# Hybrid attention and retention block: transposes on another engine, background work on another timetable, four multiplies on another engine

## The chip, the cores and the metric

The kernel runs on one core of one Trainium2 chip. The core has five engines that each work through their own queue in order and meet only at semaphores: TensorE (PE, with its weight loads shown as PEld), VectorE (DVE), ScalarE (ACT), GpSimd (POOL) and SyncE (SP, which here only issues DMAs). The metric is the device time of one execution in microseconds. Before the change the median of three runs was 1860.13 us (1857.83 to 1861.78).

## The reference, cut to what matters

One layer over 512 tokens of width 2048, float32. All mixing is causal by chunks of 64 tokens.

```python
h = rmsnorm(x, norm_gain)
proj = h @ w_in
(aq, ak, av, az, iq, ik, iw, rq, rk, rv, rz, ga, gb) = jnp.split(proj, SPLIT_POINTS, axis=-1)
...
# mixer A: an indexer scores all keys, 128 of them are kept for each query
index = jnp.einsum('bqsh,bqh->bqs', jax.nn.relu(score), w_c)
_, sel = lax.top_k(index, topk)
bias = rel_table[t5_bucket(pos_sel - pos_c[:, :, None])]
logits = jnp.einsum('bqhd,bqkhd->bqkh', q_c, k_sel) * scale + bias
...
# mixer B: retention, 8 heads of 128, chunkwise recurrent
kv = jnp.einsum('bnkhd,bnkhe->nbhde', kc * to_end[:, :, None], vc)
y = ((y - mu) * lax.rsqrt(var + EPS)).reshape(B, L, R_WIDTH) * gn_gain
...
a_out = dsa_mixer(...) * jax.nn.silu(az)
b_out = retention_mixer(rq, rk, rv, ret_gn_gain) * jax.nn.silu(rz)
merged = jax.nn.sigmoid(ga) * (a_out @ w_a_out) + jax.nn.sigmoid(gb) * (b_out @ w_b_out)
r = x + merged @ w_o
return r + (p_i @ w_ple) * jax.nn.sigmoid(r @ w_ple_gate)
```

The top-k is computed without indices: sixteen rounds, each of which finds the eight largest scores of a row and overwrites them; what was overwritten is kept, and the rest gets a large negative number in `mneg`. The position bias is computed from 32 masks per query group (position difference against a threshold) that are multiplied by a small table on PE.

## The kernel before

**Numbers.** Every float32 product is made of three products of a rounded high part and a remainder: `wh` and `wl` for weights (ACT rounds at L134, DVE or POOL subtracts at L140), `hh` and `hl` for activations. POOL subtracts for the weights of retention and of attention (`pool_units`), DVE for all others. So each 1024 columns of weights cost one ACT pass and one pass of DVE or POOL ahead of PE.

**Order.** The program order of every engine is written out by hand. PE's matmuls set the pace: after each group of three (or two) matmuls the code calls `step()`, one *tick*, which may issue other work at that point of the program. Three lists feed it: `soon` holds work due a given number of ticks later (`later(n, f)`), `todo` is a list of slots, one taken per tick, where `None` is an empty slot, and `bg` is background work. A background piece is issued in a tick when `todo` has run empty and the tick's number is a multiple of `state["rate"]`.

**Background pieces, 256 in this order.** 48 that load `x` again, normalize it (`xn`) and write the 56 sums and parts of it that the paired products use to `hd` in DRAM (`h_step`, L264 to L277); 48 top-k pieces, sixteen rounds over three query tiles of 256, 384 and 512 keys (`topk_round`, L601 and L602 on DVE, with `mneg` at the end); 160 for the bias: 128 `bias_mask` (L616, DVE) and 32 `bias_mm` (twelve matmuls, L624, an ACT copy, and a store to `scr` that ACT issues).

**Stages, in order.** The indexer's projections. Then `values` for four retention heads (64 ticks) and four heads; again `values` and four heads. A head has two projections, `ps_rq` and `ps_rk`, of 16 ticks each. `rotate` (L714 to L717, four DVE operations) follows each, and the head's remaining work goes onto `todo` only behind the second one, so that it is issued beside the next head's projections: `scores` (L747, PE; then `at`, L749, DVE), `keys` (16 stream transposes on DVE in four slots, then an ACT copy with a scale, L759), `states` (L764, PE), four `values_out` (L778 and L780, PE), `norm` (L785 to L790, DVE, and a power on POOL), `scale` (`yn`, L797, DVE), `back` (16 stream transposes, then an ACT copy with the gain, L807, and a store by SP to `yd`). Only the last head has both projections in one loop, which also reads the parts in `hd` back (`x_load`). Behind it stands gate pair 0.

22 gate pairs follow (`gemm_pair`: `rz`, `gb`, `ga` and half of `az`). A pair computes two output blocks of 128 columns with seven products of eight ticks (56 ticks) into four PSUM tiles p, v, q and r; p, v and r are used twice, so that the sixth and seventh product wait until DVE and ACT have read them (`e_d`, L229, reads r ahead of the seventh). The weights of a pair are four loads by SP and three additions by DMA that POOL issues into the loaded tile. Then branch B's projection with `w_b` (16 blocks of 8 ticks, L895), where `x` is split again on the way (`x_again`, with three empty slots behind each). Then `av` for four attention heads (64 ticks), four heads, `av`, four heads, the remaining `az`, the projections by `w_a`, eight `w_o` pairs, and the output gate.

An attention head loads its biases (`bm` from `scr`, by SP) and POOL adds `mneg` to them (L908) before DVE adds the logits. In the last four heads `a_kept` multiplies a gate that was stored in DRAM by an earlier head's output (L1002, POOL), and ACT and DVE split the result (`ah`, `al`).

**Rates.** `BG_RATE` = 2 up to the end of retention, `BG_RATE2` = 6 from there on. What is left of `bg` is issued at once behind branch B's projection.

**PSUM.** All PSUM tiles share eight banks (`P`); SBUF tiles of 512 columns share 69 slots (`U`), larger ones 5 (`B`).

Of the kernel before, what the change touches and what calls it, by code (L numbers as in the profile page):

```python
# [13 lines left out]
AF = mybir.ActivationFunctionType  # L14
# [6 lines left out]
NT = L // 128  # L21
# [13 lines left out]
def block_kernel(tc, xT, pT, posb, posq, w_in, w_v, w_ik, w_a, w_b, w_o, w_ple, w_gate,  # L35
                 w_gt, w_pt, fgb, tab, gains, cst, dec, out, out_a, out_b):
    nc = tc.nc
    pe, dve, act, pool, sp = nc.tensor, nc.vector, nc.scalar, nc.gpsimd, nc.sync

    with contextlib.ExitStack() as ctx:  # L40
# [10 lines left out]
        def U(name, dt=F32):  # L51
            return up.tile([128, L], dt, name=name, tag="u")

        def B(name, dt=F32):
            return bp.tile([128, 1280], dt, name=name, tag="b")

        def P(name):
            return pp.tile([128, L], F32, name=name, tag="p")
# [4 lines left out]
        def tok(t):  # L63
            return slice(128 * t, 128 * t + 128)
# [6 lines left out]
        unfinished = {}  # L71
        state = {"raw": 0, "split": 0, "rate": BG_RATE}
        pool_units = []
# [78 lines left out]
        todo = collections.deque()  # L152
        bg = collections.deque()
# [3 lines left out]
        def later(n, f):  # L157
            if n <= 0:
                return f()
            tick[1] += 1  # L160
            heapq.heappush(soon, (tick[0] + n, tick[1], f))

        def step():
            tick[0] += 1
            while soon and soon[0][0] <= tick[0]:
                heapq.heappop(soon)[2]()
            if todo:
                f = todo.popleft()
                if f is not None:
                    f()  # L170
            elif bg and tick[0] % state["rate"] == 0:
                bg.popleft()()

# [4 lines left out]
        def ksteps(ids):  # L178
            return [(i, k) for i in ids for k in range(units[i][2])]
# [25 lines left out]
        def gemm(ids, parts, name, c=ALL, order=None):  # L205
            return gemms([(ids, slice(0, 128), parts, c, name)], order=order)[0]
# [128 lines left out]
        ng, fg, gn = g_sb[:, 0:16], g_sb[:, 16:32], g_sb[:, 32:40]  # L335
        xs = []
        for k in range(KT):
            if k in (1, 2, 4, 8, 12):
                load_to(state["raw"] + 1)
            if k < 10:  # L340
                t = U("xk")
                sp.dma_start(t, xT[:, k, :])
                xs.append(t)
            elif k % 2 == 0:
                t = B("xk2")
# [3 lines left out]
        ident, invf, halfpi = cs[:, 0:128], cs[:, 128:129], cs[:, 129:130]  # L349
# [328 lines left out]
        def values(ids, name):  # L678

            pss = [P("ps_vn") for _ in range(NT)]  # L680
            seq = ksteps(ids)
            for s, (i, k) in enumerate(seq):
                if k == 0:
                    split_to(i + AHEAD)
                    load_to(i + AHEAD + LOADS)
                h, l = loaded[i]
                a, b = hparts[s]
                for t in range(NT):
                    pe.matmul(pss[t], a[:, tok(t)], h[:, k], start=(s == 0), stop=False)  # L689
                    pe.matmul(pss[t], a[:, tok(t)], l[:, k], start=False, stop=False)  # L690
                    pe.matmul(pss[t], b[:, tok(t)], h[:, k], start=False, stop=(s == KT - 1))  # L691
                    step()
            vs = [U(name) for _ in range(NT)]
            for t in range(NT):
                act.activation(vs[t], pss[t], AF.Copy, scale=R["nat"][:, t:t + 1])
            return vs

        def flip(dst, src, n, pairs):

            d = dst[:, 0:128 * n].rearrange("p (t q) -> p t q", q=128)  # L700
            f = src[:, 0:128 * n].rearrange("p (t q) -> p t q", q=128)
            for i in pairs:
                a, b = divmod(i, 4)
                dve.transpose(out=d[32 * a:32 * a + 32, :, 32 * b:32 * b + 32],  # L704
                              in_=f[32 * b:32 * b + 32, :, 32 * a:32 * a + 32])
# [14 lines left out]
        def retention_head(h, vs):  # L720
            hc = slice(128 * (h % 4), 128 * (h % 4) + 128)
            g128 = (1.0 - 2.0 ** (-5.0 - h)) ** 128
            dect = U("dect")
# [3 lines left out]
            else:  # L727
                i = u_r[h][0][0]
# [3 lines left out]
                pq, pk = gemms([(u, slice(0, 128), hparts, ALL, n) for u, n in zip(u_r[h], ("ps_rq", "ps_rk"))],  # L732
                               ahead=3, each=lambda s: x_load(2))
# [5 lines left out]
            if h < NH - 1:  # L739
                pk = gemm(u_r[h][1], hparts, "ps_rk")  # L740
            sk = rotate(pk)
            E = {}

            def scores():
# [5 lines left out]
                               dect[:, None, 0:128].to_broadcast([128, NT, 128]))  # L750
                E["at"] = at

            def keys(i):
                if i == 0:
                    E["kn"] = U("kn")
                if i < 4:
                    flip(E["kn"], sk, 3, range(4 * i, 4 * i + 4))
                else:
                    act.activation(E["kn"][:, 0:384], E["kn"][:, 0:384], AF.Copy, scale=dect[:, 256:257])  # L759

            def states():
                ps = P("ps_kv")
# [37 lines left out]

            def back(i):
                if i == 0:
                    E["yT"] = U("yT")
                if i < 4:
                    flip(E["yT"], E["yn"], NT, range(4 * i, 4 * i + 4))
                else:
                    act.activation(E["yT"], E["yT"], AF.Copy, scale=gn[:, h:h + 1])  # L807
                    later(2, lambda: sp.dma_start(yd[h], E["yT"]))

            todo.extend([None] * 5)  # L810
            todo.extend([scores] + [lambda i=i: keys(i) for i in range(5)] + [None] * 3 + [states, None, None])
            todo.extend([lambda t=t: values_out(t) for t in range(NT)])
            todo.extend([None, norm] + [None] * 5 + [scale] + [lambda i=i: back(i) for i in range(5)])

        Xh = {n: [None] * 8 for n in PRODUCTS}
        x_wanted = collections.deque((n, k) for n in PRODUCTS for k in range(8))
# [1 line left out]
        def x_load(count):  # L818
            while x_wanted and count:
                n, k = x_wanted.popleft()  # L820
                Xh[n][k] = U("h" + n, F32R)
                sp.dma_start(Xh[n][k].bitcast(F32), x_at[n, k])
                count -= 1
# [7 lines left out]
        hparts.clear()  # L831
        state["rate"] = BG_RATE2

# [51 lines left out]
        def x_again(k):  # L885
            xs[k] = U("xk")
            sp.dma_start(xs[k], xT[:, k, :])
            later(5, lambda: x_split(k))

        todo.extend([f for k in range(KT) for f in (lambda k=k: x_again(k), None, None, None)])  # L890
        for m in range(16):
            s = U("sg")
# [2 lines left out]
            dve.tensor_mul(s, pw, s)  # L895
            later(4, lambda m=m, s=s: sp.dma_start(mbs[m], s))
        drain()
        while bg:
            bg.popleft()()


        oTs = []
# [96 lines left out]
        def a_kept(h):  # L999
            z = U("z")  # L1000
            sp.dma_start(z, zd[h])
            later(4, lambda: pool.tensor_mul(z, z, oTs[h]))  # L1002

            def parts():
                aparts[h] = split(z, "a")

            later(6, parts)

        for h in range(NH):
            if h % 4 == 0:  # L1010
                av = values(u_av[h // 4], "av")
            if h >= NH - AZ_PAIRED:
                a_kept(h - NH + AZ_PAIRED)
            attention_head(h, av)
# [16 lines left out]
        for m in PAIRED:  # L1031
            t = B("sm")
# [18 lines left out]
        for m in range(8):  # L1051
# [13 lines left out]
            if m == 7:  # L1065
                todo.extend([None] * 24)
                for k in range(2):
                    t = U("pk")
# [9 lines left out]
        for m in range(MF):  # L1078
            i = u_p[m // 4][0]
# [3 lines left out]
            h, l = loaded[i]  # L1083
            ps = P("ps_pw")
# [7 lines left out]
            t = U("pw")  # L1092
# [157 lines left out]
RAW_BUFS = 5  # L1250
AHEAD = 4
LOADS = 2
BG_RATE = 2
BG_RATE2 = 6
X_AHEAD = 10
AZ_PAIRED = 4
WARM = 10
# [97 lines left out]
```

## Time and profile before

| | us |
|---|---|
| median of three runs | 1860.13 |
| the profiled execution | 1860.55 |
| its span, first to last instruction | 1858.8 |
| PE busy in the span | 1754.4 (94%) |
| DVE busy | 1275.8 (69%) |
| ACT busy | 738.6 (40%) |
| POOL busy | 393.7 (21%) |

A line of a timeline gives the start in the span, the duration, the engine, the line of the kernel, the operation, the tile written and those read, the shape, how many instructions were merged into the line, and in brackets how long the engine had stood idle before it and what ended that. A line of the view by stretches gives the stretch, its length, and for each engine the busy time with the number of instructions, then the granted clock of PE as a share of full speed, the share of the DMA engines and the GB/s moved. A line of the waits names the waiting engine and tile, what released it, the sum in us, how often, and the longest. In the view of one tile three durations in ns are the smallest, the median and the largest. A busy PE is not PE at its peak: its matmuls overlap, and a matmul of 512 columns that is listed with 0.39 us is followed by the next one after 0.23.

### The profile page before, as it was taken

What the parts mean: (1) busy time and instruction counts of PE and PEld (TensorE: products, weight loads), DVE (VectorE), ACT (ScalarE), POOL (GpSimd) and SP (SyncE); (2) the same over time, 40 slices, a digit from 0 to 9 for tenths busy, and PEclk for the clock granted to TensorE, in tenths of its full rate; (3) what the DMA queues carried; (4) which work ended last, traced back from release to release, by engine and by line L of the source; (5) the groups of instructions that cost most, each with busy time, mean ns of one, the idle gap of its engine ahead of it and who ended that gap; (6) DMA issues with size and microseconds to landing.
All of it is one profiled execution on the core that took longest, in us unless ns stands there. A gap on an engine that the chain in (4) does not pass through costs nothing. (4 is left out here: it accounts for less than half of the span.)

```text
span 1858.8 us, 24014 instructions
## 1 busy us (share of the span) xinstructions
PE 1754.4 (94%) x8910; PEld 1464.4 (79%) x8910; DVE 1275.8 (69%) x2211; ACT 738.6 (40%) x1087; POOL 393.7 (21%) x258
## 2 busy tenths in 40 slices
PE   8998999896889999999999999999789999999997
PEld 7987888785668777777777887888678888878887
DVE  7788778778997677777774246636657877784453
ACT  7454223123335444444552133333334444453332
POOL 2002444421121111111100044355220011111232
PEclk9999999998999999999999999999899999999999
DMA  7329335287777777877886424233235678753222
GB/s 252 112 80 332 121 112 197 80 277 243 187 201 196 189 204 199 206 201 204 220 308 214 140 82 130 88 128 114 68 105 178 170 181 202 212 161 107 95 78 93
DMA packets 115094, 309.67 MB, mean 167 GB/s; under 512 B 12832, under 2 KB 21024, under 8 KB 114976
## 3 DMA queue, kind: packets, MB, share of 16 engines
q1 hardware_dynamic: 92224, 246.25, 39.3%
q0 software_dynamic: 12960, 47.19, 14.4%
q10 hardware_dynamic: 9792, 14.68, 2.2%
q8 instruction: 70, 1.15, 0.2%
q14 instruction: 48, 0.39, 0.1%
HBM read 266.14 MB, written 41.94 MB: 166 GB/s over the span
## 5 line engine op out<-in xcount | busy, mean ns | idle before, releaser
L134 ACT ACTIVATE wh<-wraw 128x1024 fp32r<-128x1024 f32 (+2 forms) x406 | 415.0, 1040 | 599.2 <-DMA wraw<-w_in 145.0
L140 DVE TENSOR_TENSOR wl<-wraw,wh 128x1024 fp32r<-128x1024 f32 (+2 forms) x326 | 400.9, 1234 | 237.4 <-ACT wh L134 235.3
L140 POOL TENSOR_TENSOR wl<-wraw,wh 128x1024 fp32r<-128x1024 f32 x80 | 193.2, 2418 | 352.2 <-ACT wh L134 340.1
L250 PE MATMUL ps_r<-hs,wh 128*128 128x512 f32 x352 | 134.5, 418 | 17.3 <-DVE e_d L229 15.9
L105 POOL DMA_DIRECT2D wraw<-w_in x66 | 57.8, 876 | 427.4 <-DVE mk L616 144.3
L251 PE MATMUL ps_r<-hs,wl 128*128 128x256 f32 x352 | 101.7, 289 | 0.4 <-DVE wl L140 0.2
L689 PE MATMUL ps_vn<-wh,hh 128*128 128x512 f32 x256 | 100.4, 392 | 0.0
L250 PEld LDWEIGHTS ps_r<-hs,wh 128*128 128x128 f32 x352 | 69.0, 196 | 39.4 <-issue 22.1
L691 PE MATMUL ps_vn<-wh,hl 128*128 128x512 f32 x256 | 99.8, 390 | 0.0
L690 PE MATMUL ps_vn<-wl,hh 128*128 128x512 f32 x256 | 99.8, 390 | 0.0
L197 PE MATMUL ps_pg<-rh,wl 128*128 128x512 f32 x192 | 74.7, 389 | 0.0
L196 PE MATMUL ps_pg<-rl,wh 128*128 128x512 f32 x192 | 74.7, 389 | 0.0
L195 PE MATMUL ps_pg<-rh,wh 128*128 128x512 f32 x192 | 74.7, 389 | 0.0
L251 PEld LDWEIGHTS ps_r<-hs,wl 128*128 128x128 f32 x352 | 69.5, 197 | 1.7 <-DVE wl L140 1.7
L704 DVE STREAM_TRANSPOSE bm<-pn 32x320 f32<-32x320 f32 x128 | 64.3, 503 | 1.9
L105 POOL DMA_DIRECT2D wraw<-w_o x24 | 20.9, 870 | 210.9 <-DMA wraw<-w_o 101.7
L250 PE MATMUL ps_q<-ha,wh 128*128 128x512 f32 x176 | 64.5, 404 | 0.0
L250 PE MATMUL ps_v<-hs,wh 128*128 128x512 f32 x176 | 64.1, 400 | 0.0
L250 PE MATMUL ps_v<-ha,wh 128*128 128x512 f32 x176 | 64.1, 399 | 0.0
L250 PE MATMUL ps_p<-hs,wh 128*128 128x512 f32 x176 | 63.8, 399 | 0.0
L250 PE MATMUL ps_p<-ha,wh 128*128 128x512 f32 x176 | 63.7, 401 | 0.0
L251 PE MATMUL ps_v<-ha,wl 128*128 128x256 f32 x176 | 50.7, 288 | 6.0 <-DVE wl L140 6.0
(372 smaller groups left out, 4729.8 us busy)
## 6 DMA issues: line engine op xcount, KB each, us to landing
wraw<-w_in SPq DMA_DIRECT2D x174, 512.0 KB, 5.1
wraw<-w_in POOLq DMA_DIRECT2D x66, 512.0 KB, 7.2
wraw<-w_v SPq DMA_DIRECT2D x32, 512.0 KB, 3.9
wraw<-w_o SPq DMA_DIRECT2D x32, 512.0 KB, 4.9
wraw<-w_o POOLq DMA_DIRECT2D x24, 512.0 KB, 7.2
wraw<-w_gate SPq DMA_DIRECT2D x24, 512.0 KB, 4.3
hd<-hs SPq DMA_DIRECT2D x32, 256.0 KB, 4.6
hs<-hd SPq DMA_DIRECT2D x32, 256.0 KB, 5.4
```

The lines of the kernel that those rows point to most:

```text
L105: pool.dma_start(out=raw_tiles[r], in_=src[:, k0:k0 + 8, :], accum_op=OP.add)
L134: act.activation(h, raw, AF.Copy)
L140: e.tensor_sub(l, raw, h.bitcast(F32))
L195: pe.matmul(o, h[:, k, w], a, start=(s == order[0]), stop=False)
L196: pe.matmul(o, h[:, k, w], b, start=False, stop=False)
L197: pe.matmul(o, l[:, k, w], a, start=False, stop=(s == order[-1]))
L250: pe.matmul(o, h[:, k], x, start=(n < 4 and k == 0), stop=False, skip_group_check=True)
L251: pe.matmul(o[:, LO], l[:, k], x[:, LO], start=False, stop=(k == 7), skip_group_check=True)
L689: pe.matmul(pss[t], a[:, tok(t)], h[:, k], start=(s == 0), stop=False)
L690: pe.matmul(pss[t], a[:, tok(t)], l[:, k], start=False, stop=False)
L691: pe.matmul(pss[t], b[:, tok(t)], h[:, k], start=False, stop=(s == KT - 1))
L704: dve.transpose(out=d[32 * a:32 * a + 32, :, 32 * b:32 * b + 32], in_=f[32 * b:32 * b + 32, :, 32 * a:32 * a + 32])
```

## The change

Five edits.

1. `step()`: an empty slot (`None`) of `todo` counts like an empty list, so a background piece may be issued in it when the tick's number fits.
2. Retention's `keys` and `back` no longer use DVE's stream transposes. `turn` transposes on PE, three tiles for the keys and four for `yn`, into one PSUM tile `ps_t`; two slots later ACT copies it to SBUF with the same scale as before.
3. `todo` of a head: `keys` takes two slots and an empty one between them instead of five; `back` comes six slots behind `scale` instead of one, and takes two and an empty one instead of five. A head has 35 slots instead of 34.
4. Rates: 3 instead of 2 in retention, 24 instead of 6 in the gate pairs, 2 in branch B's projection, 1 from the first `av`. What is left is issued behind the first `av` and no longer ahead of it.
5. `a_kept` multiplies on DVE instead of POOL.

```diff
@@ step
-            if todo:
-                f = todo.popleft()
-                if f is not None:
-                    f()
+            f = todo.popleft() if todo else None
+            if f is not None:
+                f()
             elif bg and tick[0] % state["rate"] == 0:
                 bg.popleft()()
@@ retention_head
+            def turn(src, n):
+
+                ps = P("ps_t")
+                for t in range(n):
+                    pe.transpose(ps[:, tok(t)], src[:, tok(t)], ident)
+                return ps[:, 0:128 * n]
+
             def keys(i):
                 if i == 0:
+                    E["pk"] = turn(sk, 3)
+                else:
                     E["kn"] = U("kn")
-                if i < 4:
-                    flip(E["kn"], sk, 3, range(4 * i, 4 * i + 4))
-                else:
-                    act.activation(E["kn"][:, 0:384], E["kn"][:, 0:384], AF.Copy, scale=dect[:, 256:257])
+                    act.activation(E["kn"][:, 0:384], E["pk"], AF.Copy, scale=dect[:, 256:257])
...
             def back(i):
                 if i == 0:
+                    E["pt"] = turn(E["yn"], NT)
+                else:
                     E["yT"] = U("yT")
-                if i < 4:
-                    flip(E["yT"], E["yn"], NT, range(4 * i, 4 * i + 4))
-                else:
-                    act.activation(E["yT"], E["yT"], AF.Copy, scale=gn[:, h:h + 1])
+                    act.activation(E["yT"], E["pt"], AF.Copy, scale=gn[:, h:h + 1])
                     later(2, lambda: sp.dma_start(yd[h], E["yT"]))
 
             todo.extend([None] * 5)
-            todo.extend([scores] + [lambda i=i: keys(i) for i in range(5)] + [None] * 3 + [states, None, None])
+            todo.extend([scores, lambda: keys(0), None, lambda: keys(1)] + [None] * 3 + [states, None, None])
             todo.extend([lambda t=t: values_out(t) for t in range(NT)])
-            todo.extend([None, norm] + [None] * 5 + [scale] + [lambda i=i: back(i) for i in range(5)])
+            todo.extend([None, norm] + [None] * 5 + [scale] + [None] * 5 + [lambda: back(0), None, lambda: back(1)])
@@ branch B's projection
+        state["rate"] = 2
         todo.extend([f for k in range(KT) for f in (lambda k=k: x_again(k), None, None, None)])
...
         drain()
-        while bg:
-            bg.popleft()()
@@ a_kept
-            later(4, lambda: pool.tensor_mul(z, z, oTs[h]))
+            later(4, lambda: dve.tensor_mul(z, z, oTs[h]))
@@ attention
         for h in range(NH):
             if h % 4 == 0:
+                state["rate"] = 1
                 av = values(u_av[h // 4], "av")
+                while bg:
+                    bg.popleft()()
@@ constants
-BG_RATE = 2
-BG_RATE2 = 6
+BG_RATE = 3
+BG_RATE2 = 24
```

## The prediction

> **What bounds the kernel now.** I read the page first, then cut the span at the stages (starts of the first and last matmul of each PSUM tile), asked for the busy time of each stretch, and then for PE's waits in each.
>
> ```profile
> span 1858.8 us, 24014 instructions
> ```
> ```profile
> core 0: us, PE busy (x) PEld busy (x) DVE busy (x) ACT busy (x) POOL busy (x), PEclk, DMA share, GB/s
> 153.80:411.67 257.87, 244.69 (x1159) 204.44 (x1159) 199.69 (x491) 69.50 (x108) 104.14 (x53) 0.98 0.51 174
> 411.67:444.64 32.97, 17.58 (x94) 15.35 (x93) 26.00 (x64) 7.05 (x11) 2.23 (x3) 0.74 1.02 354
> 444.64:574.14 129.50, 112.82 (x608) 94.06 (x607) 116.93 (x221) 53.73 (x66) 26.17 (x24) 0.95 0.70 176
> 574.14:932.91 358.77, 346.14 (x2138) 281.14 (x2136) 263.36 (x390) 173.12 (x227) 40.95 (x47) 1.00 0.80 205
> 936.40:1027.00 90.60, 90.02 (x411) 72.33 (x410) 48.87 (x62) 30.54 (x38) 0.00 (x0) 1.00 0.70 241
> 1027.00:1070.00 43.00, 43.00 (x192) 35.59 (x191) 10.50 (x9) 9.69 (x10) 2.63 (x1) 1.00 0.45 152
> 1494.90:1644.95 150.05, 143.62 (x803) 122.48 (x801) 112.28 (x150) 63.16 (x75) 17.39 (x20) 1.00 0.76 195
> ```
>
> In order: retention heads; the first four products of gate pair 0 (32 ticks), with the tail of retention in them; five pairs, from one `e_d` to the sixth; sixteen pairs; branch B's projection; the first `av`; seven w_o pairs. PE bounds everywhere except in rows two and three. One w_o pair takes 150.05/7 = 21.4 us. The sixteen take 358.77/16 = 22.4, and without their 28 bias products (16.93 us, below) 21.4 too. The five take 25.9, with DVE busy 90% of it.
>
> ```profile
> PE ps_rs L747 <- DVE ra L717: 12.2, 2, 6.8
> PE ps_kv L764 <- ACT kn L759: 1.0, 1, 1.0
> ```
> ```profile
> PE ps_r L250 <- DVE e_d L229: 11.7, 4, 3.5
> ```
> ```profile
> PE ps_v L251 <- DVE wl L140: 5.1, 11, 0.6
> PE ps_r L250 <- DVE e_d L229: 4.2, 9, 0.8
> ```
>
> These are PE's waits in the heads, in the five pairs and in the sixteen (us, times, longest). In the sixteen pairs, masks included, DVE holds PE up by 9.3/16 = 0.6 us a pair; in the five, where it runs top-k rounds, for 11.7 us, and PE's clock suffers besides:
>
> ```profile
> 476.43 0.68 DVE L229 TENSOR_TENSOR e_d<-ps_r,pv 128x512 f32<-128x512 f32 x1
> ...
> 477.26 0.47 PE L250 MATMUL ps_r<-hs,wh 128*128 128x512 f32 x1 [3.53 <-DVE e_d L229]
> ...
> 526.93 0.77 PE L250 MATMUL ps_r<-hs,wh 128*128 128x512 f32 x1 [2.34 <-DVE e_d L229]
> ...
> 527.71 0.63 PE L250 MATMUL ps_r<-hs,wh 128*128 128x512 f32 x1
> ```
>
> After 3.53 us the first matmul still takes 0.47 us; after 2.34 us they take 0.77 and 0.63, the half rate. The granted clock of 0.95 over the five pairs costs 0.05 x 129.50 = 6.5 us, 1.6 for each of the four waits. The largest loss is the end of retention:
>
> ```profile
> 416.66 2.35 DVE L140 TENSOR_TENSOR wl<-wraw,wh 128x1024 fp32r<-128x1024 f32 x2
> 418.93 1.36 DVE L797 TENSOR_SCALAR yn<-ps_y,gmv,grs 128x128 f32<-128x128 f32 x4
> 420.32 5.04 DVE L704 STREAM_TRANSPOSE yT<-yn 32x128 f32<-32x128 f32 x16
> 425.40 0.72 ACT L807 ACTIVATE yT<-yT,g_sb 128x512 f32<-128x512 f32 x1 [12.38 <-DVE yT L704]
> 427.58 1.23 DVE L140 TENSOR_TENSOR wl<-wraw,wh 128x1024 fp32r<-128x1024 f32 x1 [2.22 <-ACT wh L134]
> 429.99 0.68 DVE L749 TENSOR_TENSOR at<-ps_rs,dect 128x512 f32<-128x512 f32 x1
> 430.59 4.50 DVE L704 STREAM_TRANSPOSE kn<-ra 32x96 f32<-32x96 f32 x16
> 435.12 0.61 ACT L759 ACTIVATE kn<-kn,dect 128x384 f32<-128x384 f32 x1 [3.90 <-DVE kn L704]
> 435.79 1.65 PE L764 MATMUL ps_kv<-rv,kn 128*128 128x128 f32 x6 [14.66 <-ACT kn L759]
> ```
>
> Pair 0 starts at 411.67. The flips of head 6 hold ACT for 12.38 us, ACT's late `wh` holds DVE, `at` and head 7's flips follow, and PE stands 14.66 us.
>
> **The change, part by part.** *Where the pieces go.* Background work is 256 pieces: 48 for `xn`, 48 top-k, 160 for the bias (128 masks, 32 products). A tick is one `step()`: 64 in `values`, 32 in a head, 56 in a pair, 8 in a block of B's projection. Before, a piece runs only in ticks with an empty list; a head's 34 slots fill the next head's 32 ticks, so pieces run in `values` and the head right behind it. Counting slots, 62 pieces precede the pairs, 34 top-k pieces fall into pairs 0 to 4, and masks fill the rest. After, an empty slot counts too (rate 3): 95 pieces precede the pairs, 50 run in them (rate 24), 64 beside B's projection, 47 beside the first `av`.
>
> ```profile
> L601 DVE MAX8 m<-isc x48: 413/553/689, 317.9 to 548.1; 128x8 f32<-128x256 f32 x16, 128x8 f32<-128x384 f32 x16, 128x8 f32<-128x512 f32 x16
> ...
> L602 DVE MATCH_REPLACE8 isc<-m,isc x48: 406/543/679, 318.4 to 548.9; 128x256 f32<-128x256 f32 x16, 128x384 f32<-128x384 f32 x16, 128x512 f32<-128x512 f32 x16
> ```
> ```profile
> 153.80:411.67 257.87, 59.20 (x208) 0.98 0.51 174
> ```
> ```profile
> 574.14:932.91 358.77, 16.93 (x336) 6.15 (x336) 1.00 0.80 205
> ```
> ```profile
> 574.14:932.91 358.77, 42.83 (x116) 1.00 0.80 205
> ```
>
> A top-k piece is 0.55 + 0.54 = 1.1 us. The heads gain 33 pieces, 36 us of DVE, and lose the 59.20 us of stream transposes (second row), so DVE's load there falls. The third row: the twelve matmuls of a bias product take 16.93/28 = 0.60 us of PE. By the count 8 products stay in the sixteen pairs, and 20 leave for the two later stages: 12 us out and 12 us in. The masks that run there need 88 x 42.83/116 = 32 us of DVE (fourth row), which is idle for 41.7 of 90.6 and 32.5 of 43 us. Without that cover PE would wait for at most those 32 us. ACT's stores to `scr` move along; the last falls on tick 47 of the `av` stage, and head 0's logits, which read it through `bm`'s load on SP, come 17 + 32 ticks later, 33 us, so neither SP nor POOL's mask add holds up PE. The `xn` loads and stores on SP end in the second `values`, three heads ahead of the `hd` reloads.
>
> *Transposes on PE.* Seven per head.
>
> ```profile
> 66.36 0.60 PE L489 MATMUL ps_kT<-cs,kd 128*128 128x128 f32 x4
> 66.72 0.42 PE L195 MATMUL ps_iq<-hh,wh 128*128 128x384 f32 x1
> ```
>
> Four take between 0.36 (to the next start) and 0.60 us; I take 0.44, so 0.77 a head and 6.2 us in all, wholly on PE's path. The ACT copies stay, reading PSUM. What is new is that PE, not only ACT, waits for `yn`.
>
> ```profile
> 200.67 0.89 DVE L785 BATCH_NORM_STATS2 gst<-ps_y 128x6 f32<-128x128 f32 x4 [1.14 <-PE ps_y L780]
> ...
> 203.17 1.37 DVE L797 TENSOR_SCALAR yn<-ps_y,gmv,grs 128x128 f32<-128x128 f32 x4 [1.12 <-POOL grs L790]
> ```
> ```profile
> 407.06 0.89 DVE L785 BATCH_NORM_STATS2 gst<-ps_y 128x6 f32<-128x128 f32 x4 [2.88 <-PE ps_y L780]
> ```
>
> `turn` comes 14 ticks behind the last `values_out`: 9.5 us in a head (0.67 each, from the 43.00 us of 64 `av` ticks, and a little for its other products). `yn` is complete 3.9 us behind it in the first rows (204.54 less 200.67), and so in five of the eight heads. In head 6 `scale` stands behind both `rotate`s: 13.2 us (420.29 less 407.06), and the last seven of the 14 ticks are pair ticks of 21.4/56 = 0.38, so PE asks at 411.67 + 7 x 0.38 = 414.3 and waits 6.0 us. Bounds: 0 if DVE takes `yn` first, 10 if two background pieces and a `wl` come ahead. Behind it on PE stand the products of pair 0.
>
> [...]
>
> **The sum.** *Heads.* The two long waits come from heads 0 and 4, where rate 2 piles pieces ahead of `rotate`: 12.2, 1.0 and 3.2 us of half clock (twice 1.6). At rate 3 a piece comes every 2.0 us; top-k's 1.1 fits, `xn` pieces do not quite, since they meet POOL:
>
> ```profile
> L717 DVE TENSOR_TENSOR ra<-ra,rb x16: 691/1619/2465, 170.0 to 416.0; 128x512 f32<-128x512 f32 x16
> ```
>
> The same multiply-add runs from 0.69 to 2.47 us. I take 3 us left in head 0 (0 to 5.4), 0.5 in head 4, 2.7 spread over the six heads whose DVE now takes five to ten pieces (0 to 12), and 1.5 of half clock: 7.7. The turns add 5.0. Gain 16.4 - 7.7 - 5.0 = 3.7 (bounds -5 and +11).
>
> [...]
>
> *End of retention.* 32 pair ticks at 21.4/56 make 12.2 us; `ps_rs`, `ps_kv` and `ps_y` of head 7 are 8 + 6 + 14 passes at the 0.11 of a transpose, 3.1; turns 0.8; the new wait 6.0 and its half clock 1.6: 23.7 for 32.97, gain 9.3 (5 to 15). `kn` no longer waits for DVE.
>
> *The five pairs.* Five at 21.4, two products 1.2, head 7's turn 0.4, its wait for `yn` 0.6: 109.2 for 129.50, gain 20.3 (14 to 25). Without 34 x 1.1 = 37 us of top-k DVE is busy for 80 of 109 us. *The sixteen pairs and later*: 0 (-6 to +12).
>
> *Kept gates.* Four multiplies leave POOL for DVE.
>
> ```profile
> L1002 POOL TENSOR_TENSOR z<-z,oT x4: 1288/1292/1739, 1227.9 to 1301.2; 128x512 f32<-128x512 f32 x4
> ```
> ```profile
> L669 DVE TENSOR_TENSOR aql<-aq,aqh x8: 1285/2303/2531, 1083.1 to 1324.5; 128x512 fp32r<-128x512 f32 x8
> ```
>
> 5.2 us leave POOL, and 2.8 (0.69 each) to 9.2 (the second row) enter DVE, behind which logits and softmax queue. I take 0, covered by PE's projections; uncovered it costs 5, and ACT's earlier `ah` might gain 3.
>
> Together 33.3: span 1825.5. The profiled execution ran 1860.55, 1.75 above its span, and the median of the runs is 0.4 lower: **1827**.
>
> **Rivals.** *The weight chain binds.* The sixteen pairs moved 205 GB/s at 0.80 of the DMA engines. If 22.4 a pair is the chain of loads and accumulations, masks or not, the five pairs gain 5 less and the 12 us of moved products come on top: 1827 + 17 = 1844. Against it: the w_o pairs manage 21.4 with the same loads. *Pairs quicken.* With hardly any masks all 21 could run at 20.8, which is 21.4 less the 0.6 of waits: 21 x 0.6 = 13 less, 1814. *Nothing comes of it*: top-k fills DVE in the heads as it filled it in the pairs, its 36 us reappear as waits for `sk` and `state`: 1860. Against it stand the 59.20 us. *Slower*: `turn` of `yn` stalls PE in every head, since DVE, full of pieces, and POOL, with `wl` ahead of the power, bring `yn` late. Each of seven more heads costs L + 1.6, L being the lateness past 9.5 us; from L = 3.1 (7 x 4.7 = 33) the gain is gone, and L = 4 makes 1866. Five heads with 3.9 speak against it, head 6 for it.
>
> **Chances.** Forecast 0.60 (its own range 1818 to 1836), quicker pairs 0.15, weight chain 0.13, nothing 0.04, slower 0.08. Range 1812 to 1847, which leaves out the last two and the tails. A measurement of this kernel can tell about 0.2% from no change (1856.4 to 1863.9): faster 0.88, same 0.03, slower 0.09.
>
> **What would show it.** No stream transpose left in the heads; `ps_t` waiting for `yn` some 6 us once, beside pair 0, and under 1 us elsewhere; `ps_kv` not waiting 14 us; no `e_d` wait above 1 us; pairs 1 to 5 at 21 to 22 us; half clock gone from there. I am wrong if `ps_t` waits in most heads, if `rs` waits grow, or if pairs stay above 22.

## The result, and the profile after

The changed kernel takes 1839.43 us in the median of seven runs, the kernel before 1860.13 beside it: a ratio of 0.9896 (95% interval 0.9871 to 0.9921). The forecast was 1827, its range 1812 to 1847. The direction and the range held; of the 33 us that the sum promised 21 came. The profiled execution of the changed kernel ran 1839.43:

```profile
span 1837.6 us, 23845 instructions
```

The view by stretches of the changed kernel, cut at the same marks as before, but for the second, which lies 0.16 us ahead of pair 0's first matmul (columns: stretch, length, busy time and instructions of PE, PEld, DVE, ACT and POOL, granted clock, DMA share, GB/s). In order: heads, end of retention, five pairs, sixteen pairs, branch B's projection, first `av`:

```profile
153.50:402.90 249.40, 246.79 (x1203) 206.38 (x1202) 180.89 (x387) 68.57 (x108) 104.80 (x53) 1.00 0.55 178
402.90:426.53 23.63, 18.42 (x102) 15.99 (x101) 17.11 (x33) 6.98 (x10) 1.00 (x1) 0.86 1.04 381
426.53:555.65 129.12, 112.96 (x599) 93.79 (x598) 79.33 (x103) 54.58 (x66) 27.42 (x25) 0.95 0.76 198
555.65:897.98 342.33, 330.00 (x1898) 276.60 (x1896) 234.94 (x305) 162.62 (x204) 40.90 (x47) 1.00 0.80 204
901.50:1000.20 98.70, 97.96 (x543) 73.90 (x541) 63.18 (x112) 34.52 (x49) 0.00 (x0) 1.00 0.72 243
1000.20:1054.00 53.80, 53.80 (x320) 37.63 (x313) 26.14 (x46) 16.45 (x22) 2.64 (x1) 1.00 0.52 166
```

| term of the sum | before | after | gain | forecast |
|---|---|---|---|---|
| heads | 257.87 | 249.40 | 8.5 | 3.7 |
| end of retention | 32.97 | 23.63 | 9.3 | 9.3 |
| five pairs | 129.50 | 129.12 | 0.4 | 20.3 |
| sixteen pairs and later (start of the stretch to the end of the span) | 1284.7 | 1282.0 | 2.7 | 0 |

The fourth column and 0.3 us ahead of the heads make the 21.2 us between the two spans. One row is out of line. In the five pairs DVE's load fell as foreseen, from 116.93 to 79.33 us (forecast 80), and the stretch kept its length. From one `e_d` to the next it takes 28.5, 25.7, 23.9, 24.3 and 26.8 us.

PE's waits in the changed kernel, in the heads, the end of retention, and the first and the last of the five intervals (us, times, longest):

```profile
PE ps_rs L746 <- DVE ra L716: 2.6, 1, 2.6
...
PE ps_t L756 <- DVE yn L802: 5.2, 1, 5.2
...
PE ps_t L756 <- DVE yn L802: 4.7, 1, 4.7
...
PE ps_v L249 <- ACT wh L134: 3.8, 1, 3.8
```

Waits on `e_d` are no longer than 0.3 us among the five; a weight part, `wh`, is waited for in their place.

**Another cut.** `e_d` stands in the middle of a pair. In pair 0 it starts 0.2 us behind the first matmul of the fifth product in both kernels (444.64 and 444.44 before, 426.53 and 426.33 after), so the 9.3 us are real, and the row of the five pairs begins with the last three products of pair 0. The sixth `e_d` comes some 4 us behind PE in both kernels. Cut at the start of each pair's first matmul into `ps_p` instead, the view by stretches of the kernel before, and of the changed one, gives pair 0 (with the end of retention in it) and pairs 1 to 5:

```profile
411.67:452.76 41.09, 25.70 (x141) 22.43 (x140) 33.56 (x85) 8.05 (x11) 3.94 (x4) 0.79 0.89 297
452.76:578.49 125.73, 109.05 (x586) 90.77 (x585) 112.41 (x205) 52.73 (x65) 25.34 (x23) 0.95 0.73 186
```
```profile
403.06:442.88 39.82, 29.93 (x152) 25.51 (x151) 25.20 (x47) 12.45 (x16) 4.79 (x5) 0.83 0.96 324
442.88:560.03 117.15, 105.67 (x574) 87.94 (x573) 73.97 (x94) 50.09 (x62) 24.50 (x22) 0.97 0.76 197
```

Pair 0 gained 1.3 us, pairs 1 to 5 8.6. Five pairs at the forecast's 21.4 would be 107.0. The single pairs 1 to 5 of the changed kernel run 19.8, 21.7, 23.9, 24.3 and 27.5: the loss sits in the last three. Before, pair 1 alone took 28.6, so the whole gain is in it; pairs 2 to 5 took 97.2 us and take 97.4.

**Where pair 0 lost its gain.** Its last three products, from `e_d` to pair 1, take 16.3 us instead of 8.1. In them stand the wait of 4.7 us for head 7's `yn`, its four transposes, and matmuls at half rate behind the wait (0.63 us until 440, granted clock 0.50 from 434 to 440). What held `yn`, by the timeline of the changed kernel:

```profile
432.02 0.95 POOL L105 DMA_DIRECT2D wraw<-w_in  x1 [25.49 <-DMA wraw<-w_in]
432.68 1.37 POOL L795 TENSOR_TENSOR grs<-grs,mhalf 128x4 f32<-128x4 f32 x1
```
```profile
434.08 1.37 DVE L802 TENSOR_SCALAR yn<-ps_y,gmv,grs 128x128 f32<-128x128 f32 x4 [4.26 <-POOL grs L795]
```

DVE had the variances ready at 426.5. The power that `yn` needs stands in POOL's queue behind an addition into a weight tile, which POOL issues only when the load into that tile has landed, and POOL stood 25.49 us for it. Before the change this addition went out at 439.96, and the power, at 444.38, waited for DVE alone. The same row holds the power up in e1, e6, e9 and e12 below, with POOL idle for 24 to 26 us ahead of it; no run moved it, so how much the wait would shrink without it stays open.

**The suspect.** The first four pairs (`rz`) multiply their gate on POOL (`go`) and store it to `bd` from SP (L859 before, L863 after); all later pairs store from ACT. SP also issues the weight loads (L116). SP's longest wait in pairs 1 to 5, of the kernel before and of the changed one:

```profile
SPq L859 <- POOL go L858: 73.5, 8, 19.4
```
```profile
SPq L863 <- POOL go L862: 64.7, 8, 17.9
```

What SP issues around the start of pair 4 of the changed kernel (508.3), and what POOL, ACT and PE do behind it, by the timeline:

```profile
492.89 0.33 SPq L863 DMA_DIRECT2D bd<-go  x1
493.31 0.38 SPq L116 DMA_DIRECT2D wraw<-w_in  x1
496.31 0.33 SPq L863 DMA_DIRECT2D bd<-go  x1
496.69 1.61 SPq L867 DMA_DIRECT2D y<-yd  x2
498.40 1.74 SPq L116 DMA_DIRECT2D wraw<-w_in  x3
...
506.05 1.79 POOL L105 DMA_DIRECT2D wraw<-w_in  x2 [9.77 <-DMA wraw<-w_in]
...
511.58 2.00 ACT L134 ACTIVATE wh<-wraw 128x1024 fp32r<-128x1024 f32 x2 [6.20 <-DMA wraw<-w_in]
...
512.69 0.50 PE L249 MATMUL ps_v<-hs,wh 128*128 128x512 f32 x1 [1.42 <-ACT wh L134]
```

SP stands until `go` of pair 2 is there. Behind the first store leaves the last load of pair 3, behind the second store and the `y` loads the first three of pair 4, in a burst; only then can POOL issue the addition into the second of them (506.05), ACT round the sum, and PE begin the second product of pair 4, 1.42 us late. A pair later the same chain ends in a longer wait, and PE's matmuls of 512 columns behind it take 0.63 us, not 0.40, until 546:

```profile
538.27 2.00 ACT L134 ACTIVATE wh<-wraw 128x1024 fp32r<-128x1024 f32 x2 [10.36 <-DMA wraw<-w_in]
...
539.38 0.66 PE L249 MATMUL ps_v<-hs,wh 128*128 128x512 f32 x1 [3.81 <-ACT wh L134]
...
541.02 0.63 PE L249 MATMUL ps_v<-hs,wh 128*128 128x512 f32 x1
```

### The profile page after: what moved, and what is told of

Its sections match the earlier page's. It is cut to its first block, busy times and chain, and to the rows that moved or that the text cites. A ratio compares the mean times of both kernels' runs of the same rounds, so it can differ in the third digit from the quotient of the medians.

```text
span 1837.6 us, 23845 instructions
## 1 busy us (share of the span) xinstructions
PE 1760.4 (96%) x8966; PEld 1466.5 (80%) x8966; DVE 1218.1 (66%) x1959; ACT 739.7 (40%) x1087; POOL 389.6 (21%) x254
## 4 chain that ended last, share of the span: by engine, by line
PE 55%; DMA 21%; DVE 13%; issue 5%; ACT 4%; POOL 1%; SPq 0%; POOLq 0%; ACTq 0%; DVEq 0%
DMA wraw<-w_in 15%; DMA wraw<-w_o 5%; DVE wl L140 4%; PE ps_vn L688 3%; PE ps_w L194 3%; PE ps_vn L689 3%; PE ps_vn L690 3%; ACT wh L134 3%; PE ps_w L195 3%; PE ps_w L196 3%; PE ps_pg L196 2%; PE ps_pg L195 2%; PE ps_pg L194 2%; DVE bm L703 2%; PE ps_rk L194 2%
## 5 line engine op out<-in xcount | busy, mean ns | idle before, releaser
L249 PE MATMUL ps_r<-hs,wh 128*128 128x512 f32 x352 | 128.3, 403 | 4.2 <-DVE e_d L228 3.7
L249 PEld LDWEIGHTS ps_r<-hs,wh 128*128 128x128 f32 x352 | 66.4, 189 | 24.3 <-issue 6.5
L249 PE MATMUL ps_v<-hs,wh 128*128 128x512 f32 x176 | 67.9, 420 | 6.5 <-ACT wh L134 6.5
L911 POOL TENSOR_TENSOR bm<-bm,mneg 128x1280 f32<-128x1280 f32 x8 | 21.4, 2673 | 180.6 <-DMA bm<-scr 180.6
```

The lines of the kernel that those rows point to most:

```text
L249: pe.matmul(o, h[:, k], x, start=(n < 4 and k == 0), stop=False, skip_group_check=True)
```

## The experiments

Theory S: the loads of the next pair are held in SP's in-order queue behind a store that waits for `go`, and that sets the pace of these pairs. Rivals: D, the DMA engines need that long; P, POOL's multiplies and accumulating transfers set the pace; V, the prediction's own, DVE does; later Q, it helps merely to use two queues. Twelve runs were made in three groups, each group on one chip with the kernel before beside it; e11 is the changed kernel once more, and e12 is e1 once more. All stretches are in us and from one profiled execution each; "heads" goes from the last matmul of the first `values` to pair 0, pairs by the starts of their first matmuls, the last column from the second to the sixth `e_d` (the measure that the expectations use).

| | ratio to before (95%) | heads | pair 0 | pairs 1-5 | pairs 6-20 | 2nd to 6th `e_d` |
|---|---|---|---|---|---|---|
| before | 1 | 257.9 | 41.1 | 125.7 | 335.3 | 97.7 |
| changed | 0.9896 (0.9871-0.9921) | 249.6 | 39.8 | 117.2 | 319.4 | 100.6 |
| e1_store_act | 0.9870 (0.9842-0.9898) | 249.6 | 40.1 | 107.3 | 321.5 | 87.4 |
| e2_before_store_act | 0.9954 (0.9932-0.9975) | 258.7 | 41.3 | 122.2 | 331.8 | 93.8 |
| e3_before_few_topk | 0.9922 (0.9892-0.9952) | 250.0 | 40.5 | 119.6 | 336.6 | 96.8 |
| e4_turns_only | 1.0017 (0.9999-1.0035) | 268.8 | 40.3 | 120.0 | 339.2 | 99.6 |
| e5_timetable_only | 1.0045 (1.0029-1.0061) | 264.4 | 41.0 | 122.4 | 325.8 | 99.7 |
| e6_two_stores_act | 0.9906 (0.9876-0.9936) | 251.2 | 37.3 | 109.0 | 321.5 | 89.7 |
| e7_stores_act_late_turn | 0.9899 (0.9878-0.9921) | 251.2 | 36.3 | 113.1 | 319.4 | 90.0 |
| e8_kept_pool | 0.9924 (0.9899-0.9950) | 249.6 | 38.0 | 117.2 | 317.6 | 100.7 |
| e9_store_late_sp | 0.9857 (0.9836-0.9878) | 251.1 | 39.2 | 107.0 | 323.2 | 87.5 |
| e10_store_early_sp | one run | 251.0 | 37.2 | 119.0 | 323.0 | 100.6 |
| e11_changed_again | 0.9925 (0.9912-0.9938) | 251.2 | 39.9 | 116.1 | 323.1 | 99.1 |
| e12_store_act_again | 0.9855 (0.9841-0.9870) | 251.2 | 37.4 | 106.4 | 322.5 | 85.9 |

The two kernels that stand twice in the table show how far two executions differ: 1 us in pairs 1 to 5, but 2.7 in pair 0 and 3.7 in pairs 6 to 20. So the 1.3 us that pair 0 gained can't be told from nothing.

**The stores from ACT's queue (e1, e12).**

```diff
-                later(8, lambda: sp.dma_start(bd[2 * n + i], o))
+                later(8, lambda: act.dma_start(bd[2 * n + i], o))
```

> The changed kernel with the stores of bd issued from ACT's queue instead of SP's, so that no weight load of the next pair stands behind a store that waits for POOL's go. Theory S (in the four pairs that store bd, SP's in-order queue holds the loads of the next pair behind the store, and that sets 24 us a pair whatever DVE does): the three intervals between e_d of pairs 1 to 4 fall from 25.7, 23.9 and 24.3 to 21 to 22 us, the stretch of five pairs from 129 to 118 to 122, the time from 1839 to 1829 to 1833. Rival D (the DMA engines, busy 0.73 to 0.78 there, need that long): intervals and time unchanged within 1 us and 3 us. Rival P (POOL's muls and accumulating transfers set the pace): unchanged too, since both stay where they are.

Pairs 1 to 5 fell to 107.3, the measure of the expectation to 87.4 from 100.6. D and P expected no change and are out: the same bytes move, POOL does the same work in the same order. The time in that group (median 1839.91, against 1862.55 for before, with 1829 to 1833 expected) was too loose to tell it from the changed kernel, so it was run once more beside the changed kernel itself.

> The stores of bd issued from ACT, once more, beside the changed kernel on the same chip. Theory S: stretch from the second to the sixth e_d 86 to 91, time 4 to 12 us below the changed kernel of the same call. If the gain of the stretch is given back later: time within 3 us of it.

> The changed kernel unaltered, for the comparison on this chip: ratio to the kernel before 0.987 to 0.992; stretch from the second to the sixth e_d 99 to 102.

On one chip the changed kernel took 1845.76 and this one 1831.86 us (before 1858.64): 13.9 us less, with intervals that do not touch, and 1.9 more than the expectation allowed. The profiled executions differ by 9.7 us in pairs 1 to 5 and 2.5 in pair 0; e1, the same kernel as e12, does not have the latter. The stretch, by its view in the run beside the changed kernel, works without half clock:

```profile
443.54:549.97 106.43, 102.50 (x575) 85.70 (x573) 74.93 (x95) 48.21 (x60) 24.76 (x22) 1.00 0.83 213
```

The DMA engines move 213 GB/s here, more than the 197 with which the pairs had taken 117: on average they had room, and waited for issues.

**Later and earlier in SP's own queue (e9, e10).** These keep the queue and move only the place of the store in it: e9 as shown, e10 with 1 tick for 8.

```diff
-                later(8, lambda: sp.dma_start(bd[2 * n + i], o))
+                later(30, lambda: sp.dma_start(bd[2 * n + i], o))
```

> The changed kernel with the stores of bd still in SP's queue, but issued 22 ticks later there (some 8 us of a pair), behind the next weight loads instead of ahead of them. Theory S in its strict form (loads are held because they stand behind a store whose go is not ready): SP's wait on go falls from 64.7 us to under 15, the stretch from the second to the sixth e_d from 100.6 to 86 to 91, as with the stores on ACT, and the time by 5 to 12 us against the changed kernel of the same call. Rival Q (two queues instead of one are what helped): 97 to 101, no change in time.

> The changed kernel with the stores of bd in SP's queue, issued 7 ticks earlier. Theory S: SP meets the store sooner and holds the loads at least as long, the same stretch is 100 to 106 for 100.6. Rival Q: 100 to 101.

With the store 22 ticks later, SP still issues it, and pairs 1 to 5 take 107.0; 7 ticks earlier they take 119.0, about as the changed kernel; by its own measure, 100.6 us, that run fits S and Q alike and decides nothing. The later store decides: it is the place in the queue, not the queue, and Q is out. The stretch and SP's waits of the later store:

```profile
445.47:552.49 107.02, 102.15 (x575) 85.53 (x574) 74.43 (x93) 48.33 (x61) 25.26 (x22) 1.00 0.81 211
```
```profile
SPq L863 <- POOL go L862: 33.8, 8, 9.9
```

One number of S missed: 33.8 us of waiting for `go` are left, not under 15. The length of the wait is no measure, then; what counts is which loads stand behind it. Around the start of pair 4 of this kernel (508.0) the timeline shows:

```profile
482.65 0.48 SPq L116 DMA_DIRECT2D wraw<-w_in  x1
491.88 0.32 SPq L863 DMA_DIRECT2D bd<-go  x1
495.84 0.33 SPq L116 DMA_DIRECT2D wraw<-w_in  x1
496.98 0.32 SPq L863 DMA_DIRECT2D bd<-go  x1
499.54 5.19 SPq L116 DMA_DIRECT2D wraw<-w_in  x3
...
501.15 0.90 POOL L105 DMA_DIRECT2D wraw<-w_in  x1 [4.20 <-DMA wraw<-w_in]
```

The program order now has the first load of pair 4 ahead of these stores (482.65) and the second, into which POOL adds, between them. The addition goes out at 501.15 instead of 506.05, 4.9 us sooner though this kernel is 2 us behind at the start of pair 3 (486.4 against 484.4), and PE begins the second product of pair 4 without a wait. The median of 1831.05 us is 14.7 below the changed kernel of the same group, where 5 to 12 were expected.

**Two bounds in the kernel before (e2, e3).** e2 makes the edit of e1 in the kernel before. e3 leaves out fifteen of the sixteen top-k rounds, so it no longer selects the keys, and keeps the slots:

```diff
-            dve.max(m8, a)
-            dve.match_replace(out=a, in_to_replace=m8, in_values=a, imm_value=-3.39e38)
             if last:
+                dve.max(m8, a)
+                dve.match_replace(out=a, in_to_replace=m8, in_values=a, imm_value=-3.39e38)
```

> The kernel before with the stores of bd issued from ACT's queue, its top-k rounds still beside the pairs. If the loads behind the store and DVE's top-k were two bounds of nearly the same length there (theory S with a second bound): the stretch of 129.5 us falls by 0 to 5 only, to 124 to 130, with e_d waits still above 5 us; time 1857 to 1862. If SP's queue alone had set it before: 118 to 122, time 1852. If DVE alone: 129 to 130, time 1860.

> The kernel before with only the last of the 16 top-k rounds computed; the slots of the other rounds stay, empty, so that everything else keeps its place (the selection is left out). Theory S: DVE's busy time in the five pairs falls by about 35 us, the e_d waits vanish, and the stretch of 129.5 us still stays at 122 to 130, because the loads bind at about 24 a pair; time 1850 to 1860. Rival V, the prediction's own (DVE binds there): the stretch falls to about 109 and the time to 1836 to 1842.

```profile
453.32:575.54 122.22, 107.26 (x587) 89.65 (x585) 112.67 (x206) 53.96 (x67) 25.33 (x23) 0.96 0.75 193
```
```profile
443.89:563.49 119.60, 108.08 (x586) 89.61 (x585) 80.33 (x112) 52.84 (x65) 25.29 (x23) 0.96 0.75 195
```

These are pairs 1 to 5 of e2 and of e3; the stretch of 129.5 us of the expectations is 125.9 in e2 and 124.0 in e3. Without the store alone they fall by 3.5 us, without DVE's top-k alone by 6.1 (DVE's busy time from 112.41 to 80.33); with both gone, in e9 and e12, by 19 (with the other edits of the change). While one bound stands, removing the other shows a fraction of what the two together hold. e3's time fell further than S expected (1849.29 for 1850 to 1860), because the heads, too, gained 8 us without top-k (PE's waits for `rotate` there fall from 12.2 to 5.4 us), which the expectation left out. e2's time, 1848.74 us, lies below the 1857 to 1862 expected; on its chip the kernel before took 1854.59, and the gain of 0.5% is still more than the 3.5 us; pairs 6 to 20, without an edit, are 3.5 shorter as well, which is within what two executions of a kernel differ, and the rest wasn't followed.

**The parts alone (e4, e5).** e4 has the kernel before with `turn` in `keys` and `back`, in the old slots; e5 has the new `step`, the four rates and the later flush, and the stream transposes on DVE.

> The kernel before with the TensorE transposes of the change alone, in the slots of before; no timetable, flush or kept-gates edit. By the prediction's terms: heads lose the 5.0 us of turns and gain what the flips cost DVE in waits (0 to 16), the end of retention falls from 33.0 to 20 to 25, the five pairs stay at 125 to 130 with their top-k rounds, all later stages unchanged: 1847 to 1856. If the flips were hidden everywhere but at the end: 1855. If all of the change's gain came from its timetable: 1860.

> The kernel before with the timetable alone (background in empty slots at rate 3, then 24, 2 and 1, the remainder issued beside the first av) and the stream transposes left on DVE. Theory S: heads get slower, as top-k joins the 59 us of flips (250 to 265 us), the end of retention stays near 33, the five pairs stay at 125 to 130, sixteen pairs 342, B's projection 98 and av 53: 1855 to 1870. Rival V: five pairs at 109 to 114, time 1838 to 1850.

Alone, e4 gains nothing (1867.00 us, above all its expectations) and e5 loses 0.45% (1870.63, just above S's 1855 to 1870), while the whole change gains 1.0%. The answer is in the heads, 268.8 and 264.4 us for 257.9. Heads of e4, with PE's waits, and the first of PE's waits in the heads of e5:

```profile
153.70:421.90 268.20, 253.32 (x1201) 211.31 (x1200) 141.50 (x282) 68.67 (x108) 103.61 (x53) 0.97 0.50 166
```
```profile
PE ps_rs L747 <- DVE ra L717: 11.9, 2, 6.5
PE ps_t L757 <- DVE yn L803: 3.0, 1, 3.0
```
```profile
PE ps_kv L763 <- ACT kn L758: 14.5, 5, 8.4
```

e4 keeps the two waits for `rotate`, since the background still piles up in heads 0 and 4; it pays for the turns and gets a wait for `yn`, which stands one slot ahead of its turn there. DVE has 58 us less to do in the heads, and none of it was on the path there. e5 has one of these waits left, 2.6 us, but top-k now stands in front of the flips, and PE waits for `kn` five times. The turns make the room into which the timetable puts its work: only the two together pay.

**SP's other store, and the waits for `yn` (e6, e7).** e6 also issues the store of `yT` from ACT; e7 adds fifteen empty slots ahead of the turn in heads 6 and 7:

```diff
-                    later(2, lambda: sp.dma_start(yd[h], E["yT"]))
+                    later(2, lambda: act.dma_start(yd[h], E["yT"]))
...
-            ... + [scale] + [None] * 5 + [lambda: back(0), None, lambda: back(1)])
+            ... + [scale] + [None] * (5 if h < 6 else 20) + [lambda: back(0), None, lambda: back(1)])
```

> The changed kernel with the stores of bd and also those of yd issued from ACT's queue, so that in pair 0 no load stands behind the store that waits for head 7's yT. Theory S: the wait of 10.5 us in SP's queue on yT goes, the interval from the first to the second e_d falls from 28.5 (32.6 with bd's stores alone on ACT) to 24 to 27, the five pairs from 129 to 112 to 117, time 1828 to 1834. Rival D: five pairs unchanged within 2 us of the run with bd's stores on ACT (120), time 1834 to 1840.

> As the run with both stores on ACT, and in the last two heads the turn of yn comes 15 ticks later. If PE's waits for yn (5.2 beside pair 0, 4.7 in the stretch after) only stand there because the turn is asked for early: both waits fall under 1 us, their half clock goes too, end of retention 16 to 18.5 for 23.6, five pairs another 5 to 7 less than without it; time 1818 to 1826. If the loads bind there anyway, the waits come back on wh or wl and the time stays within 3 us of the run without it.

e6 shows nothing beyond e1 and e12: SP's wait for `yT` goes, but the first interval is 29.7 us and the five pairs are 119.4, as rival D had it, and the last column stays at 89.7. So S was wrong for this store: it held no load that PE needed soon. In e7 the wait of 5.2 us for `yn` goes and others come, 2.6 us on `yn` of head 7 and a long one:

```profile
PE ps_kv L769 <- ACT kn L764: 9.4, 1, 9.4
```

The moved slots put head 7's `kn` behind another `wh` on ACT, and for that one ACT waits 9.75 us, for a weight load that by its place in the order is the one SP issued at 423.26 among the reloads from `hd`. From 406 to 428 these leave SP about every 0.7 us, and from 406 to 422 the DMA share is 1.05 at 390 GB/s (in the changed kernel's end of retention, second row of the first view above, 1.04 at 381). Pairs 0 and 1 together take 59.8 us in e7, 57.1 in e6, and 59.6 in the changed kernel. The time, 1835.66 us, is not the 1818 to 1826 hoped for but within 3 us of e6's 1834.57, which the expectation had for loads that bind anyway. So the wait for `yn` in pair 0 seems to lie over a transfer that would be waited for next; what a turn alone moved, without head 7's list moving along, wasn't tried.

**The kept gates back on POOL (e8).**

```diff
-            later(4, lambda: dve.tensor_mul(z, z, oTs[h]))
+            later(4, lambda: pool.tensor_mul(z, z, oTs[h]))
```

> The changed kernel with the four kept-gate multiplies back on POOL. The prediction costs the move at 0, with bounds of 5 lost and 3 gained: time 1834 to 1844, most likely equal to the changed kernel's within 2 us; the stretch from the first attention head to the start of the second projection stays at 321 within 2 us if the edit is hidden, 318 if it cost 3, 324 if it gained 3.

From the first attention head to the second projection the trace has 322.1 us with POOL and 321.2 with DVE: hidden, as costed.

## Why the prediction was partly right

The time lies inside the range, and 21 of the 33 us came, but not where the sum had them. The largest term gave 0.4 us for 20.3; that the heads gave 4.8 more than forecast and the later stages 2.7 made up for part of it, and that was luck.

*Heads: mechanism right, one term too large.* The waits that a piece every 2 us leaves were put at 7.7; the trace has one of 2.6 and a clock of 1.00. 257.87 - 16.4 + 2.6 leaves 244.1, and the 249.40 measured put the turns at 5.3, where the forecast had 5.0 (a remainder, with the 16.4 as the forecast reckoned them). DVE's load fell as argued, from 199.69 to 180.89. What the forecast called meeting POOL is in the trace of before: the multiply-add takes 0.69 us at 326.72, with POOL idle, and 2.46 at 248.25, beside a subtraction of POOL from 247.76 to 250.16.

*End of retention: right, and lost again behind its mark.* `yn` is late by 5.2 us for 6.0, and the stretch is 23.63 for 23.7. Of the 9.3 us gained pair 0's remaining products lost 8.2: they met head 7's wait for `yn`, 4.7 us where the forecast had 0.6, with half clock behind it. The forecast took the 3.9 us from the first statistics to `yn` that most heads need. Here they are 10.3 (425.13 to 435.45), since POOL's power stands behind an addition that waits for a load (POOL idle for 25.49 us ahead of it); the forecast did not look at POOL's queue there.

*The five pairs: the step that failed.* "Five at 21.4" for a gain of 20.3. The forecast saw DVE at 90%, PE waiting for `e_d`, and concluded that a pair without top-k runs like a `w_o` pair. What it didn't ask is what else had to be ready then. SP's waits, 73.5 us on `go`, stood in the trace of before; they were passed over because SP does nothing but issue transfers. But here its wait held the loads that stood behind it: in the changed kernel SP waits 64.7 us on `go`, and with that store moved behind weight loads (e9) pairs 1 to 5 take 107.0 us for the 116.1 of e11. The forecast's own sign, pairs 1 to 5 at 21 to 22 us without half clock, failed: they take 23.4 on average, with a clock of 0.97. With the store out of the way, pairs 1 to 5 take 106.4 to 107.3 in three runs (e1, e9, e12), and 5 x 21.4 is 107.0: the size was right for a kernel without the second bound. (e6 takes 109.0; e7, whose turn falls into pair 1, 113.1.) That is 10 of the 20 us that this row missed. Most of the other 10 are the last three products of pair 0, which belong to the row and for whose turn and wait the forecast had 1.0; without SP's store the row by the forecast's own marks is still 116.8 to 120.1 in those three runs, for 109.2.

*The rival "weight chain binds"* had the right kind of cause at the wrong place. It charged all 21 pairs; the loads bind only where SP stores. Its refutation, that the `w_o` pairs manage 21.4 with the same loads, fails since SP has no such store there.

*The rival "pairs quicken"* did not come: with hardly any masks the sixteen pairs run at 342.33/16 = 21.4, not 20.8, and PE's waits in them are 11.3 us for 9.3 before. Nor did *slower*: in the heads PE never waits for `yn`, only beside pair 0.

*Sixteen pairs and later: right in the sum, wrong in the price.* The pairs lost 16.4 us for the 12 reckoned, and the two later stages grew by 8.1 and 10.8. The busy time of the twelve matmuls, 0.60 us a product, was the wrong price. The bias products in the sixteen pairs, beside branch B's projection and beside `av` (busy time of PE, then of ACT), and one of them among its neighbours, in the changed kernel:

```profile
555.65:897.98 342.33, 2.97 (x96) 2.20 (x8) 1.00 0.80 204
901.50:1000.20 98.70, 7.43 (x156) 5.06 (x12) 1.00 0.72 243
1000.20:1054.00 53.80, 8.52 (x128) 6.26 (x11) 1.00 0.52 166
```
```profile
1019.93 0.39 PE L690 MATMUL ps_vn<-wh,hl 128*128 128x512 f32 x1
1020.25 0.83 PE L623 MATMUL ps_bias<-mk,d 128*32 128x512 bf16 x12
1021.01 0.50 PE L688 MATMUL ps_vn<-wh,hh 128*128 128x512 f32 x1
1021.36 0.40 PE L689 MATMUL ps_vn<-wl,hh 128*128 128x512 f32 x1
```

Matmuls of this stage start 0.23 us apart (1021.60 to 1021.83 and on); the three starts around the product take 1.43 instead of 0.47, so a product of 512 columns costs 0.96. The narrow ones, of 128 columns, are first in the list and stay in the pairs; the wide ones moved. And 13 and 11 ran later where 2 had before: 18.9/22 = 0.86 each. The move loses 2.5 us; that this term still ended at 2.7 of gain comes from stretches with the same code on PE (the `w_o` pairs took 147.25 us for 150.05, attention 321.2 for 322.6), and why they were shorter stays open; pairs 6 to 20 of the changed kernel took 319.4 and 323.1 us in two executions, so it may be no more than such a spread.

*Kept gates: 0, right.*

## What to carry to other kernels

Before an engine at 90% is called the bound, take its work away on paper and follow the next pair through every queue that feeds it, one that only issues transfers too; two bounds looked like one here (3.5 and 6.1 us for removing either, 19 with both gone). On a queue that issues both loads and stores, place a store behind the loads that others wait for: here one number, 8 ticks made 30, was worth 0.8% (14.7 of 1845.76 us). And look at what stands just behind a stretch's last mark: the 9.3 us gained in one stretch were real, and 8.2 of them were spent again in the next three products.

## What the runs showed of the hardware that was not expected

Transfers that add into a loaded tile were dear here. The view of the transfers in pairs 1 to 5 of the changed kernel, by queue (packets, MB, share of the 16 engines' time) and by what issued them:

```profile
q1 hardware_dynamic: 5151, 15.12, 38.0%
q0 software_dynamic: 1994, 7.25, 36.0%
...
wraw<-w_in SPq DMA_DIRECT2D x22, 512.0 KB, 5.9
wraw<-w_in POOLq DMA_DIRECT2D x14, 512.0 KB, 6.4
```

POOL's fourteen additions (the 7.25 MB of the second queue) take nearly as much of the engines' time as all that SP issues (the first queue), with half the bytes, and each adds 6.4 us, in the median from issue to landing, to the chain from a load to its product.

PE's wait of 3.81 us at the second product of pair 5 of the changed kernel cost about double: behind it the matmul pairs start 0.64 us apart (541.02 to 541.66) instead of 0.36 until 546, some 3 us more (the granted clock is 0.50 from 540 to 545). In e1, e6 and e9, with the store moved, PE waits for weights there 1.1 us at most, and the granted clock is 1.00 over the whole stretch (in e12 too). In the kernel before, all four waits for `e_d` were followed by half rate, the one of 3.53 us too, whose first matmul still took 0.47 us: the granted clock was 0.50 from 479 to 482, and behind the waits of 3.50, 2.34 and 2.37 us from 503 to 506, 527 to 529 and 554 to 557. Beside pair 1 of e7 PE waits 2.6 us, and the granted clock is 1.00 over pairs 1 to 5.
